# Attention with the values held still and the probabilities streamed, two heads on the column halves of the matrix engine

## The chip, the core and the metric

The kernel runs on one core of a Trainium2 chip. The core has a matrix engine (TensorE, PE in the rows; its weight loads are PEld), a vector engine (VectorE, DVE), a scalar engine (ScalarE, ACT), GpSimd (POOL), and a sync engine (SP) that issues the DMAs. Operands lie in SBUF, matmul results in PSUM, which has eight banks of 128 partitions by 512 fp32 numbers. A matmul holds one operand still in the array (the stationary one, loaded first) and streams the other through it (the moving one). The metric is the device time of one execution, in microseconds; less is better.

## The reference, cut to what matters

The program is one block of another design (a recurrence, a differential attention, an MLP) followed by two transformer layers on 256 tokens of width 1024. Each of the two layers is half an FFN, an attention of 16 heads of 64, and half an FFN again. The change is in those two attentions alone. Cut down, they compute:

```python
q, k, v = split(xn @ w_in, 3)                    # 16 heads of 64; xn is 256 x 1024
# layer 0, heads 0-7 (stick breaking)
z = q @ k.T * scale
between = sums of log_sigmoid(-z) over the later keys, strictly causal
out = exp(log_sigmoid(z) + between) @ v          # these weights need no normalisation
# layer 0, heads 8-15 ("moba": with 256 tokens there is one block, so plain causal softmax)
# layer 1, heads 0-7 ("forget": causal softmax, logits + c_q - c_k)
# layer 1, heads 8-15 ("dilated": softmax over window keys, each weighted by a count 1..3)
p = softmax(logits); out = p @ v
x = x + concat(out) @ w_out
```

## The kernel before, in words

The kernel is one long instruction stream for TensorE in an order fixed when the program is built; the other engines are placed around it by a scheduler. The dense products (weights in fp32, split into a high and a low part so that three one-pass matmuls replace an exact one, `mm3`) form the main stream. Attention is written as side streams (Python generators) that a planner, `Weave`, slips between the matmuls of the main stream. The planner keeps a clock `W.t` made of its own estimates (`mm` adds `2 * max(n, m) / 1.2` ns for an exact fp32 product with `m` stationary and `n` moving columns, times `share`); a side stream says how long it wants to be left alone (`yield 3.0` is 3 us by that clock) or what it waits for, and takes its PSUM bank with `sbank`.

The 16 heads of a layer come in four groups of four heads. For each group the main stream makes q and k (`queries`) and v (`values`), and side streams do the rest:

- `softmax_side`, one stream per group and per block `t` of 128 queries: logits by four matmuls, mask added by matmul, row maximum (DVE), exponent with row sums (ACT), transposes of the unnormalised probabilities on TensorE (L707) and their copy to SBUF (ACT, L709). Then the values product (L721 to L723): for each of four heads and each of `t + 1` blocks of 128 keys one exact fp32 matmul, whose stationary operand is the transposed 128 x 128 probability block and whose moving operand is the head's 64 columns of v. The output is 128 queries by 4 x 64. It is multiplied by the reciprocal sums into a tile `o` (DVE, L727), and `out_side` (L650) transposes `o` in two blocks back to a feature-major layout, from which `dst` copies it to `oT` or, for the last group, splits it for the output projection.
- `stick_group` with two `stick_pair` streams per group: the two heads of a pair each take three such matmuls (L771 to L773), the group's results are copied to two tiles `o` (ACT, L785), and each goes through `out_side`.

In the profile all matmuls but transposes carry line L287 and all transposes line L291, so the tiles tell them apart: `b<-v,w` is a values product, `b<-ident,o` a transpose of an output, `b<-ident,w` a transpose of probabilities (or of q and k), `b<-hi,hTh`, `lo,hTh` and `hi,hTl` are the three products of the main stream. An exact fp32 matmul leaves two records in the profile, a transpose one.

Of the kernel before, what the change touches and what calls it, by code (L numbers as in the profile page):

```python
# [7 lines left out]
F32 = mybir.dt.float32  # L8
# [4 lines left out]
AF = mybir.ActivationFunctionType  # L13
ALU = mybir.AluOpType
# [204 lines left out]
class Ker:  # L219
# [427 lines left out]
        self.w2.put(i, 0.0)  # L647
        return 0.8

    def out_side(self, o, dst):  # L650

        b = yield from self.sbank()
        for k in range(2):
            self.tr(b[1][:, k * 128:(k + 1) * 128], o[:, k * 128:(k + 1) * 128])
        dst(b[1][:, :256].rearrange("p (a b) -> p a b", b=128))
        self.sdrop(b, 1.6)

    def softmax_side(self, pool, t, wait, lhs, rhs, vm, mask, cnt, dst):

        nc = self.nc  # L660
# [23 lines left out]
        for par in range(2):  # L684
# [9 lines left out]
                    nc.vector.scalar_tensor_tensor(out=pp[:, i, :nk], in0=pp[:, i, :nk], scalar=1.0, in1=cnt[:, 256 - nk:], op0=ALU.mult, op1=ALU.mult, accum_out=l[:, h:h + 1])  # L694
                P[h] = pp[:, i]
            self.sdrop(bs[par], 2.2 + par)
        yield 3.0 if cnt is None else 4.2
        PT = {}
        blocks = [(h, b) for h in (0, 2, 1, 3) for b in range(t + 1)]
        pts = []  # L700
# [10 lines left out]
            self.w2.put(held.pop(0), 0.0)  # L711
        for i in held:
            self.w2.put(i, 0.0)
        rl = pool.tile([128, 4], F32, name="rl", tag="rl", bufs=4)
        nc.vector.reciprocal(out=rl, in_=l)
        yield [vm]
        yield 0.8
        vt = vm.res
        ab = yield from self.sbank()
        av = ab[1][:, :256].rearrange("p (h d) -> p h d", d=64)  # L720
        for h in (0, 2, 1, 3):  # L721
            for b in range(t + 1):
                self.mm(av[:, h], PT[h, b], vt[b][:, h * 64:h * 64 + 64], b == 0, b == t)  # L723
        for k in pts:
            self.w2.put(k, 0.0)
        o = pool.tile([128, 256], F32, name="o", tag="o", bufs=3)
        nc.vector.tensor_tensor(out=o.rearrange("p (h d) -> p h d", d=64), in0=av, in1=rl.unsqueeze(2).to_broadcast([128, 4, 64]), op=ALU.mult)  # L727
        self.sdrop(ab)
        yield 1.0
        yield from self.out_side(o, dst[t])  # L730
        return 1.6

    def stick_pair(self, pool, j, ab, wait, kT, qT, vm):

        nc, mm = self.nc, self.mm
        yield wait
        bs = yield from self.sbanks()
        hs = (2 * j, 2 * j + 1)
        zs = [b[1][:, :384] for b in bs]
        for a, b, first in ((0, 0, True), (128, 256, False)):  # L740
            for z, h in zip(zs, hs):
                mm(z[:, b:b + 256 - a], kT(h, a, a + 128), qT(h, a, 256), first, True, True, 0.5)
        diag = [b[1].rearrange("p (a k) -> p a k", k=256)[:, :, 0:128] for b in bs]
        self.add_mask(diag, self.A["stick"], lambda x: x.unsqueeze(1).to_broadcast([64, 2, 128]))
        sp = []
        for z in zs:
            e = pool.tile([128, 384], F32, name="e", tag="e", bufs=2)
            nc.scalar.activation(out=e, in_=z, func=AF.Abs)
            self.act_pinned(out=e, in_=e, func=AF.Exp, scale=-1.0)
            self.act_pinned(out=e, in_=e, func=AF.Ln, bias=1.0)  # L750
            i, w = yield from self.w2.get()
            nc.vector.scalar_tensor_tensor(out=w[:, :384], in0=z, scalar=0.0, in1=e, op0=ALU.max, op1=ALU.add)
            sp.append((i, w))
        yield 4.6
        for z, (i, w) in zip(zs, sp):
            mm(z[:, 0:256], self.A["nsuf"], w[:, 0:256], False, True, True)
            mm(z[:, 128:256], self.A["nones"], w[:, 256:384], False, True, True)
            mm(z[:, 256:384], self.A["nsuf"], w[:, 256:384], False, True, True)
            self.w2.put(i, 0.0)
        ws = []  # L760
        for b, z in zip(bs, zs):
            i, w = yield from self.w2.get()
            self.act_pinned(out=w[:, :384], in_=z, func=AF.Exp)
            self.sdrop(b, 1.0)
            ws.append((i, w))
        yield [vm]
        yield 1.6
        vt = vm.res
        for h, (i, w) in zip(hs, ws):
            vs = slice(h * 64, h * 64 + 64)  # L770
            mm(ab[:, 0, h], w[:, 0:128], vt[0][:, vs], True, True)  # L771
            mm(ab[:, 1, h], w[:, 128:256], vt[0][:, vs], True, False)
            mm(ab[:, 1, h], w[:, 256:384], vt[1][:, vs], False, True)  # L773
            self.w2.put(i, 0.0)

    def stick_group(self, pool, wait, kT, qT, vm, dst):
        b = yield from self.sbank()
        ab = b[1].rearrange("p (t h d) -> p t h d", t=2, d=64)
        heads = [self.W.spawn(self.stick_pair(pool, j, ab, wait, kT, qT, vm)) for j in range(2)]
        yield heads  # L780
        os = []
        for t in range(2):
            o = pool.tile([128, 256], F32, name="o", tag="o", bufs=3)
            os.append(o)
            self.nc.scalar.activation(out=o.rearrange("p (h d) -> p h d", d=64), in_=ab[:, t], func=AF.Copy)  # L785
        self.sdrop(b)
        yield 0.9
        for t in range(2):
            yield from self.out_side(os[t], dst[t])
        return 1.6  # L790

    def attn_layer(self, pool, hT, layer, after):
# [1070 lines left out]
```

## Time and profile before

| | us |
|---|---|
| median of 3 timed runs | 1516.84 (1516.67 to 1520.73) |
| the profiled execution | 1517.79 |
| its span, first to last instruction | 1516.0 |
| TensorE busy in the span | 1473.4 (97%) |
| VectorE, ScalarE busy | 927.7 (61%), 760.7 (50%) |
| attention of layer 0, and of layer 1 (with the norm before it) | about 680 to 812, and 1188 to 1320 |

A row of instructions names the source line, the engine, the operation, the tiles written and read, for TensorE the stationary shape as rows*columns and then the moving shape, and the count of records. Matmul records overlap, since they are pipelined, so the rate of a stream is read from the starts of its records, not from their lengths.

### The profile page before, as it was taken

Reading aid. Unit: us, or ns where it says so; the run is one execution under the profiler, and the core shown is the slowest. Engines: PE = TensorE matmul, PEld = TensorE weight load, DVE = VectorE, ACT = ScalarE, POOL = GpSimd, SP = SyncE. Lnnn points to the kernel's source line nnn. Section 1 sums busy time; section 2 is a strip of 40 time slices with the busy share of each in tenths; the row PEclk is TensorE's granted clock in tenths of the full one; section 3 lists DMA queues with packets and bytes.
Section 4 is the critical chain, followed back from the end, with each engine's and each line's share of the span. In section 5 each row is a group of like instructions: output and inputs, shape, how many; then the busy total and the mean of one; then the engine's idle time right before and its main releaser. Section 6 shows DMA issues by size and latency. Waiting matters only on the chain.

```text
span 1516.0 us, 22441 instructions
## 1 busy us (share of the span) xinstructions
PE 1473.4 (97%) x8804; PEld 1235.3 (81%) x8804; DVE 927.7 (61%) x1529; ACT 760.7 (50%) x1142; POOL 46.9 (3%) x70
## 2 busy tenths in 40 slices
PE   7899988999999999999999999999999999999999
PEld 6887767888888778887888888887888878888887
DVE  5885778755558755558546554565545787565552
ACT  6644445544446544436665444445444566464441
POOL 1120100000000000001100000000000010000000
PEclk9999999999999999999999999999999999999999
DMA  7233338655554765545434756547565444276551
GB/s 254 87 121 108 101 113 272 203 191 187 181 167 140 229 204 193 186 145 195 137 101 140 220 184 196 187 146 235 183 195 189 139 158 128 82 223 193 177 186 55
DMA packets 76298, 254.97 MB, mean 168 GB/s; under 512 B 11040, under 2 KB 13344, under 8 KB 76192
## 3 DMA queue, kind: packets, MB, share of 16 engines
q1 hardware_dynamic: 76192, 253.53, 51.8%
q8 instruction: 69, 1.13, 0.3%
q14 instruction: 37, 0.30, 0.1%
HBM read 252.45 MB, written 1.05 MB: 167 GB/s over the span
## 4 chain that ended last, share of the span: by engine, by line
PE 79%; DVE 7%; DMA 6%; ACT 5%; issue 2%; SPq 0%; POOL 0%; ACTq 0%; DVEq 0%; POOLq 0%
PE b L287 75%; DMA raw<-in_w_dram 5%; PE b L291 4%; DVE lo L374 3%; ACT hi L373 2%; DMA grow<-in_norm_mix_g_dram 0%; DMA stage<-in_consts_dram 0%; DMA lam<-in_lam_k_dram 0%; ACT L380 0%; DVE c L1141 0%; POOL rb L572 0%; DVE U L1269 0%; POOL rb L571 0%; DVE u L1138 0%; ACT e L384 0%
## 5 line engine op out<-in xcount | busy, mean ns | idle before, releaser
L374 DVE TENSOR_TENSOR lo<-raw,hi 128x1024 fp32r<-128x1024 f32 (+1 forms) x465 | 562.0, 1215 | 356.1 <-ACT hi L373 347.1
L373 ACT ACTIVATE hi<-raw 128x1024 fp32r<-128x1024 f32 (+1 forms) x465 | 486.0, 1050 | 415.8 <-PE b L287 207.1
L287 PE MATMUL b<-hi,hTh 128*128 128x512 f32 (+2 forms) x1312 | 495.6, 378 | 0.5 <-ACT hi L373 0.5
L287 PE MATMUL b<-lo,hTh 128*128 128x512 f32 (+2 forms) x1312 | 484.7, 369 | 0.8 <-DVE lo L374 0.8
L287 PE MATMUL b<-hi,hTl 128*128 128x512 f32 (+2 forms) x1312 | 484.9, 370 | 0.1
L287 PEld LDWEIGHTS b<-hi,hTl 128*128 128x128 f32 x1312 | 247.5, 189 | 43.1 <-DVE hTl L374 0.6
L287 PEld LDWEIGHTS b<-hi,hTh 128*128 128x128 f32 x1312 | 247.6, 189 | 42.0 <-issue 2.7
L287 PEld LDWEIGHTS b<-lo,hTh 128*128 128x128 f32 x1312 | 248.0, 189 | 40.0 <-DVE lo L374 1.7
L287 PE MATMUL b<-hi,aTh 128*128 128x512 f32 x480 | 191.4, 399 | 0.0
L287 PE MATMUL b<-lo,aTh 128*128 128x512 f32 x480 | 187.3, 390 | 0.0
L287 PE MATMUL b<-hi,aTl 128*128 128x512 f32 x480 | 187.2, 390 | 0.0
L287 PEld LDWEIGHTS b<-hi,aTl 128*128 128x128 f32 x480 | 90.2, 188 | 19.8
L287 PEld LDWEIGHTS b<-lo,aTh 128*128 128x128 f32 x480 | 90.3, 188 | 17.4
L287 PEld LDWEIGHTS b<-hi,aTh 128*128 128x128 f32 x480 | 90.2, 188 | 17.5
L471 ACT ACTIVATE a<-b,rsi_x 128x512 f32<-128x512 f32 (+1 forms) x52 | 34.4, 662 | 54.0 <-PE b L287 54.0
L373 ACT ACTIVATE aTh<-b 128x512 fp32r<-128x512 f32 (+1 forms) x64 | 36.3, 567 | 39.5 <-PE b L291 38.5
L473 DVE SCALAR_TENSOR_TENSOR a<-b,rsi_x,a 128x512 f32<-128x512 f32 (+1 forms) x52 | 37.3, 717 | 28.4 <-PE b L287 15.9
L287 PE MATMUL b<-hi,hT1h 128*128 128x512 f32 (+1 forms) x128 | 53.5, 418 | 0.0
L374 DVE TENSOR_TENSOR aTl<-b,aTh 128x512 fp32r<-128x512 f32 (+1 forms) x64 | 41.8, 653 | 17.2 <-ACT aTh L373 16.9
L287 PE MATMUL b<-lo,hT1h 128*128 128x512 f32 (+1 forms) x128 | 47.7, 372 | 0.6 <-DVE lo L374 0.6
L287 PE MATMUL b<-hi,hT1l 128*128 128x512 f32 (+1 forms) x128 | 47.4, 371 | 0.0
L374 DVE TENSOR_TENSOR hTl<-b,hTh 128x512 fp32r<-128x512 f32 (+1 forms) x48 | 29.2, 619 | 23.5 <-ACT hTh L373 23.5
(583 smaller groups left out, 1289.0 us busy)
## 6 DMA issues: line engine op xcount, KB each, us to landing
raw<-in_w_dram SPq DMA_DIRECT2D x446, 512.0 KB, 4.2
raw<-in_w_dram SPq DMA_DIRECT2D x16, 384.0 KB, 3.4
grow<-in_norm_ffn_dram SPq DMA_DIRECT2D x4, 512.0 KB, 5.0
x<-in_x_dram SPq DMA_DIRECT2D x4, 256.0 KB, 5.5
x<-in_x_dram SPq DMA_DIRECT2D x2, 512.0 KB, 4.3
grow<-in_norm_mix_dram SPq DMA_DIRECT2D x2, 512.0 KB, 4.5
out_dram<-x SPq DMA_DIRECT2D x4, 256.0 KB, 2.0
raw<-in_w_dram SPq DMA_DIRECT2D x2, 396.0 KB, 3.5
```

The costliest lines, as they stand in the source:

```text
L287: self.nc.tensor.matmul(out=out, lhsT=lhsT, rhs=rhs, start=start, stop=stop, skip_group_check=skip)
L291: self.nc.tensor.transpose(out=out, in_=src, identity=self.ident)
L373: self.nc.scalar.activation(out=hi, in_=src, func=AF.Copy)
L374: self.nc.vector.tensor_tensor(out=lo, in0=src, in1=hi.bitcast(F32), op=ALU.subtract)
L471: nc.scalar.activation(out=a[t], in_=p, func=AF.Silu if kind == "swiglu" else AF.Relu, scale=hT[t].r)
L473: nc.vector.scalar_tensor_tensor(out=a[t], in0=p, scalar=hT[t].r, in1=a[t], op0=ALU.mult, op1=ALU.mult)
```

## The change

The values product is turned round: v becomes the stationary operand (128 keys by the 64 columns of one head) and the transposed probabilities the moving one (128 columns, or 256 in the stick groups). The output is then feature-major: 64 partitions by 128 queries. Two heads of a pair are written to the two partition halves of one PSUM bank, so each matmul addresses 64 of the array's 128 columns. Since the sums are then along the wrong axis of the output, the probabilities are divided before they are transposed: one `reciprocal` and four scalings by a row factor, two on ACT and two on DVE. `o`, its scaling and copies, and `out_side` are gone; `dst` reads the PSUM bank directly. The planner's clock gets `share` 0.5 for the new matmuls, and the wait before the transposes is 1 us longer.

```diff
--- before.py
+++ after.py
@@ -647,14 +647,6 @@
         self.w2.put(i, 0.0)
         return 0.8
 
-    def out_side(self, o, dst):
-
-        b = yield from self.sbank()
-        for k in range(2):
-            self.tr(b[1][:, k * 128:(k + 1) * 128], o[:, k * 128:(k + 1) * 128])
-        dst(b[1][:, :256].rearrange("p (a b) -> p a b", b=128))
-        self.sdrop(b, 1.6)
-
     def softmax_side(self, pool, t, wait, lhs, rhs, vm, mask, cnt, dst):
 
         nc = self.nc
@@ -694,7 +686,15 @@
                     nc.vector.scalar_tensor_tensor(out=pp[:, i, :nk], in0=pp[:, i, :nk], scalar=1.0, in1=cnt[:, 256 - nk:], op0=ALU.mult, op1=ALU.mult, accum_out=l[:, h:h + 1])
                 P[h] = pp[:, i]
             self.sdrop(bs[par], 2.2 + par)
-        yield 3.0 if cnt is None else 4.2
+        rl = pool.tile([128, 4], F32, name="rl", tag="rl", bufs=4)
+        nc.vector.reciprocal(out=rl, in_=l)
+        for h in (0, 2, 1, 3):
+            p = P[h][:, :nk]
+            if h % 2:
+                nc.vector.tensor_scalar(out=p, in0=p, scalar1=rl[:, h:h + 1], scalar2=None, op0=ALU.mult)
+            else:
+                nc.scalar.activation(out=p, in_=p, func=AF.Copy, scale=rl[:, h:h + 1])
+        yield 4.0 if cnt is None else 5.2
         PT = {}
         blocks = [(h, b) for h in (0, 2, 1, 3) for b in range(t + 1)]
         pts = []
@@ -711,26 +711,23 @@
             self.w2.put(held.pop(0), 0.0)
         for i in held:
             self.w2.put(i, 0.0)
-        rl = pool.tile([128, 4], F32, name="rl", tag="rl", bufs=4)
-        nc.vector.reciprocal(out=rl, in_=l)
         yield [vm]
         yield 0.8
         vt = vm.res
         ab = yield from self.sbank()
-        av = ab[1][:, :256].rearrange("p (h d) -> p h d", d=64)
-        for h in (0, 2, 1, 3):
-            for b in range(t + 1):
-                self.mm(av[:, h], PT[h, b], vt[b][:, h * 64:h * 64 + 64], b == 0, b == t)
+        av = ab[1][:, :256].rearrange("p (j q) -> p j q", q=128)
+        for b in range(t + 1):
+            for j in range(2):
+                for par in range(2):
+                    h = 2 * j + par
+                    self.mm(av[64 * par:64 * par + 64, j], vt[b][:, h * 64:h * 64 + 64], PT[h, b], b == 0 and j == 0, b == t and j == 1, True, 0.5)
         for k in pts:
             self.w2.put(k, 0.0)
-        o = pool.tile([128, 256], F32, name="o", tag="o", bufs=3)
-        nc.vector.tensor_tensor(out=o.rearrange("p (h d) -> p h d", d=64), in0=av, in1=rl.unsqueeze(2).to_broadcast([128, 4, 64]), op=ALU.mult)
-        self.sdrop(ab)
-        yield 1.0
-        yield from self.out_side(o, dst[t])
+        dst[t](av)
+        self.sdrop(ab, 1.6)
         return 1.6
 
-    def stick_pair(self, pool, j, ab, wait, kT, qT, vm):
+    def stick_pair(self, pool, j, ab, begun, wait, kT, qT, vm):
 
         nc, mm = self.nc, self.mm
         yield wait
@@ -766,27 +763,23 @@
         yield [vm]
         yield 1.6
         vt = vm.res
-        for h, (i, w) in zip(hs, ws):
-            vs = slice(h * 64, h * 64 + 64)
-            mm(ab[:, 0, h], w[:, 0:128], vt[0][:, vs], True, True)
-            mm(ab[:, 1, h], w[:, 128:256], vt[0][:, vs], True, False)
-            mm(ab[:, 1, h], w[:, 256:384], vt[1][:, vs], False, True)
+        first = not begun
+        begun.append(j)
+        for b in range(2):
+            for par, (i, w) in enumerate(ws):
+                h = 2 * j + par
+                mm(ab[64 * par:64 * par + 64, j, 128 * b:256], vt[b][:, h * 64:h * 64 + 64], w[:, 256 * b:256 + 128 * b], first and b == 0, b == 1 and not first, True, 0.5)
+        for i, w in ws:
             self.w2.put(i, 0.0)
 
     def stick_group(self, pool, wait, kT, qT, vm, dst):
         b = yield from self.sbank()
-        ab = b[1].rearrange("p (t h d) -> p t h d", t=2, d=64)
-        heads = [self.W.spawn(self.stick_pair(pool, j, ab, wait, kT, qT, vm)) for j in range(2)]
-        yield heads
-        os = []
-        for t in range(2):
-            o = pool.tile([128, 256], F32, name="o", tag="o", bufs=3)
-            os.append(o)
-            self.nc.scalar.activation(out=o.rearrange("p (h d) -> p h d", d=64), in_=ab[:, t], func=AF.Copy)
-        self.sdrop(b)
-        yield 0.9
-        for t in range(2):
-            yield from self.out_side(os[t], dst[t])
+        ab = b[1].rearrange("p (j q) -> p j q", q=256)
+        begun = []
+        yield [self.W.spawn(self.stick_pair(pool, j, ab, begun, wait, kT, qT, vm)) for j in range(2)]
+        for t in range(2):
+            dst[t](ab[:, :, t * 128:t * 128 + 128])
+        self.sdrop(b, 1.6)
         return 1.6
 
     def attn_layer(self, pool, hT, layer, after):
```

In the built program the DMA queue and GpSimd have the same instructions in the same order as before. TensorE's stream differs only inside the two attentions: 96 values matmuls become 88 (24 + 48 of the softmax streams as before, 16 instead of 24 of the stick streams), and 32 transposes of outputs are gone. The 88 stand in 15 places, 8 with four and 7 with eight, between other work each time.

The first place is the first values product of layer 0 (heads 8 to 11, queries 0 to 127). TensorE before; `w__6941` holds the transposed probabilities:

```order
L287 MATMUL b<-hi,hTl 128x512
L287 MATMUL b<-v,w__6941 128x64 x4
L287 MATMUL b<-hi,hTh 128x512
L287 MATMUL b<-lo,hTh 128x512
L287 MATMUL b<-hi,hTl 128x512
...
L291 MATMUL b<-ident,o 128x128 x2
```

TensorE now, at the same place (`w__6950` is the same tile under another number):

```order
L287 MATMUL b<-hi,hTl 128x512
L287 MATMUL b<-w__6950,v 64x128 x4
L287 MATMUL b<-hi,hTh 128x512
L287 MATMUL b<-lo,hTh 128x512
L287 MATMUL b<-hi,hTl 128x512
```

The four matmuls now write 64 partitions by 128 columns instead of 128 by 64, they alternate between the lower and the upper half of the bank, and the two transposes that followed are gone.

The second place is the first stick group of layer 0, where the two pairs finish. TensorE before (`w__7199` and `w__7201` are the weights of the two heads of a pair, `w__7212` and `w__7214` of the other pair):

```order
L287 MATMUL b<-v,w__7199 128x64 x3
L287 MATMUL b<-v,w__7201 128x64 x3
L287 MATMUL b<-hi,hTh 128x512
...
L287 MATMUL b<-v,w__7212 128x64 x3
L287 MATMUL b<-v,w__7214 128x64 x3
```

TensorE now:

```order
L287 MATMUL b<-w__7197,v 64x256
L287 MATMUL b<-w__7199,v 64x256
L287 MATMUL b<-w__7197,v 64x128
L287 MATMUL b<-w__7199,v 64x128
L287 MATMUL b<-hi,hTh 128x512
...
L287 MATMUL b<-w__7210,v 64x256
L287 MATMUL b<-w__7212,v 64x256
L287 MATMUL b<-w__7210,v 64x128
L287 MATMUL b<-w__7212,v 64x128
```

Six matmuls of a pair have become four, two of them 256 columns wide, and the two heads alternate.

The third place is the start of layer 1's attention, where little work is ready. TensorE before, from the transposes of q and k (`w__11120`) over those of the first probabilities (`w__11211`, `w__11212`, dilated heads) to the next logits (`qkT`):

```order
L291 MATMUL b<-ident,w__11120 128x128 x4
L287 MATMUL b<-hi,hTh 128x512
L287 MATMUL b<-lo,hTh 128x512
L287 MATMUL b<-hi,hTl 128x512
L291 MATMUL b<-ident,w__11211 128x128 x2
L291 MATMUL b<-ident,w__11212 128x128 x2
L287 MATMUL b<-qkT 128x256 x4
```

TensorE now (`w__11088` are q and k, `w__11179` the first of the probabilities):

```order
L291 MATMUL b<-ident,w__11088 128x128 x4
L287 MATMUL b<-hi,hTh 128x512
L287 MATMUL b<-lo,hTh 128x512
L287 MATMUL b<-hi,hTl 128x512
...
L287 MATMUL b<-qkT 128x256 x4
...
L291 MATMUL b<-ident,w__11179 128x128 x2
```

The transposes of the probabilities have moved behind the next logits and their masks, and six matmuls of the main stream instead of three stand ahead of those logits.

## Rows read from the trace of the kernel before

**Rows 1.** Page, busy time of each engine; granted TensorE clock in 40 slices (tenths).

```profile
PE 1473.4 (97%) x8804; PEld 1235.3 (81%) x8804; DVE 927.7 (61%) x1529; ACT 760.7 (50%) x1142; POOL 46.9 (3%) x70
...
PEclk9999999999999999999999999999999999999999
```

**Rows 2.** Page, chain of work that ended last, by engine.

```profile
PE 79%; DVE 7%; DMA 6%; ACT 5%; issue 2%; SPq 0%; POOL 0%; ACTq 0%; DVEq 0%; POOLq 0%
```

**Rows 3.** Stretches: length; busy PE, PEld, DVE, ACT, POOL; clock, DMA share, GB/s.

```profile
680.00:812.00 132.00, 128.82 (x812) 111.23 (x811) 75.97 (x121) 80.42 (x165) 9.16 (x8) 0.99 0.39 128
1188.00:1320.00 132.00, 127.89 (x798) 110.38 (x797) 91.69 (x210) 77.71 (x168) 8.81 (x8) 1.00 0.40 130
```

**Rows 4.** Waits of TensorE in layer 0, then layer 1: total us, times, longest.

```profile
PE b L291 <- DVE qss L558: 2.0, 1, 2.0
...
PE b L291 <- DVE w__11212 L694: 0.6, 1, 0.6
```

**Rows 5.** Timeline of TensorE, layer 0: start us, length us, instruction, stationary, moving.

```profile
714.71 0.40 PE L287 MATMUL b<-hi,hTl 128*128 128x512 f32 x1
714.95 1.00 PE L287 MATMUL b<-v,w__6941 128*128 128x64 f32 x8
...
716.07 0.39 PE L287 MATMUL b<-lo,hTh 128*128 128x512 f32 x1
...
716.99 0.39 PE L287 MATMUL b<-hi,hTl 128*128 128x512 f32 x1
717.22 0.38 PE L291 MATMUL b<-ident,o 128*128 128x128 f32 x2
...
717.68 0.39 PE L287 MATMUL b<-lo,hTh 128*128 128x512 f32 x1
```

**Rows 6.** Timeline of TensorE in the recurrence, 64-column matmuls between full ones.

```profile
130.39 0.40 PE L287 MATMUL b<-hi,hT1l 128*128 128x512 f32 x1
130.72 0.45 PE L287 MATMUL b<-UV,G 128*64 128x64 f32 x4
131.00 0.39 PE L287 MATMUL b<-S,AR 128*64 128x128 f32 x2
131.22 0.39 PE L287 MATMUL b<-UV,G 128*64 128x64 f32 x4
131.45 0.38 PE L287 MATMUL b<-S,AR 128*64 128x128 f32 x2
...
132.10 0.40 PE L287 MATMUL b<-lo,hT1h 128*128 128x512 f32 x1
```

**Rows 7.** Timeline in the recurrence, weight loads beside matmuls.

```profile
141.66 0.20 PEld L287 LDWEIGHTS b<-S,AR 128*64 128x64 f32 x2
141.72 0.39 PE L287 MATMUL b<-S,AR 128*64 128x128 f32 x2
141.83 0.36 PEld L287 LDWEIGHTS b<-UV,G 128*64 128x64 f32 x4
```

**Rows 8.** Timeline of TensorE, layer 0, logits on the row halves.

```profile
712.86 1.13 PE L287 MATMUL b<-qkT 64*128 64x256 f32 x8
713.82 0.38 PE L287 MATMUL b<-cb_causal,cb_identb 64*128 64x256 bf16 x4
```

**Rows 9.** Timeline of TensorE, layer 0, an exact matmul with 256 moving columns.

```profile
736.43 0.59 PE L287 MATMUL b<-w__7124,c_nsuf 128*128 128x256 f32 x2
736.86 0.38 PE L287 MATMUL b<-w__7124,c_nones 128*128 128x128 f32 x2
```

**Rows 10.** Groups by line: busy us, mean ns of one, idle before it.

```profile
L374 DVE TENSOR_TENSOR lo<-raw,hi 128x1024 fp32r<-128x1024 f32 (+1 forms) x465 | 562.0, 1215 | 356.1 <-ACT hi L373 347.1
...
L727 DVE TENSOR_TENSOR o<-b,rl 128x256 f32<-128x256 f32 x12 | 5.1, 422 | 4.9 <-PE b L287 4.7
...
L715 DVE RECIPROCAL rl<-l 128x4 f32<-128x4 f32 x12 | 2.1, 175 | 5.3 <-ACT w__7427 L384 1.5 <-ACT w__12156 L384 1.4 <-ACT w__11606 L384 1.4
...
L614 ACT ACTIVATE w__6994<-b,rsi_x 128x256 f32<-128x256 f32 x1 | 0.5, 474 | 0.0
```

## The prediction

> **What bounds the kernel now.** I read the page's busy times first, then the chain, then the two attentions as stretches, then the waits, and last the timeline of the places that change. TensorE is busy 97% of the span and its clock is at the full level in every slice [rows 1]; 79% of the chain that ended last is TensorE [rows 2]. That is an average over stages, so the attentions are read by themselves: in each, TensorE is busy 128 of 132 us, while DVE and ACT have 58 to 70% at most and the DMA engines 40% [rows 3]. The few idle microseconds of TensorE there stand at the start of a layer and end on the preparation of q and k (2.0 us in layer 0); the only wait that ends on a softmax is one of 0.6 us [rows 4]. So a microsecond of TensorE work taken out of an attention should shorten the program by about a microsecond, as long as nothing new comes late.
>
> **What goes on TensorE.** The unit to compare with is the main stream: from 716.07 to 716.99 four records start, 0.23 us each [rows 5]. From 714.71 to 716.07 lie two such steps and the four values matmuls of four heads (eight records): 1.36 - 0.46 = 0.90 us, or 0.225 us a matmul [rows 5]. Before the change there are 24 of 96 such matmuls in fours: 6 softmax streams with one key block (24 matmuls), 6 with two (48), 4 pairs of stick heads with six (24). 96 / 4 x 0.90 = 21.6 us. The transposes of the outputs: from 716.99 to 717.68 lie two steps and two transposes, 0.69 - 0.46 = 0.23 us [rows 5]; 32 of them, 16 x 0.23 = 3.7 us. Together 25.3 us go.
>
> **What comes on TensorE.** The new shape, 64 stationary columns and 128 moving ones, is in the trace, in the recurrence: `S,AR` takes 0.22 us for its two records (131.00 to 131.22), as long as the old shape, because now the moving side sets the pace [rows 6]. With 256 moving columns an exact matmul takes 0.43 us (736.43 to 736.86) [rows 9]. So one matmul by itself gains nothing; the gain is that two heads, on different column halves, run at the same time. No row shows two column halves side by side: in the recurrence a run stays on one half. The nearest rows are the row halves: eight records of logits with 256 moving columns, four matmuls of 0.43 us, take 0.96 us from 712.86 to the next kind at 713.82, where one after the other they would take 1.72 [rows 8, 9]. The bounds are therefore 0.22 us a pair (at the same time) and 0.44 (in turn). I take the first, since the rows next to it run in parallel, and since two exact streams together ask for no more than the trace already shows: one has 128 columns in 0.11 us a record [rows 6], so two of them have 256, and the main stream's 512 columns in 0.23 us are the same rate [rows 5].
> The softmax streams then have 6 x 2 + 6 x 4 = 36 pairs x 0.22 = 7.9 us, the stick pairs 4 x (0.43 + 0.22) = 2.6 us, together 10.5.
> TensorEngine Tiling (Array Packing) in the Trainium skill says under Key Properties that different tiles can load and multiply in parallel; TensorE: Matmul & The Clock Gate, also of the Trainium skill, gives in Part 3 (Packing small matmuls) a measured speedup of 2.38 for three column tiles. No run here shows either. By 2.38 out of 3 a pair would cost 0.28 us, the 10.5 would be 13.2, and the gain 2.7 us less.
>
> **What the switch costs.** Going to 64 columns and back is not free. From 130.39 to 132.10 lie two main steps (0.46), eight records of `UV,G` at 0.23 us per four, and two `S,AR` at 0.22 (0.90 in all): 1.71 - 0.46 - 0.90 = 0.35 us are left, between the last full matmul and the second one after [rows 6]. A values product of the old shape has no such remainder: its eight records take eight times the 0.11 us. The order of the new program has 15 such places, 15 x 0.35 = 5.25 us. For four matmuls that means 2 x 0.22 + 0.35 = 0.79 against 0.90: nearly the whole gain is eaten; for eight, 1.23 against 1.80. A bound from the other side is the same remainder with two halves to load, 0.05 more each (the first four `UV,G` take 0.28 instead of 0.23 [rows 6]): 6.0 us.
> The sum on TensorE: 25.3 - 10.5 - 5.25 = 9.5 us less.
>
> **What moves on the other engines.** DVE loses 12 `o` scalings of 0.42 us [rows 10] and gets 24 of a probability tile, which lies in SBUF and is at most as large; ACT gets 24, at most 0.47 us each by the nearest row [rows 10], and loses four copies. In the attentions ACT rises by at most 6 us per 132 and DVE by less than 3, and neither comes near full [rows 3]. No DMA moves.
> The new wait is that the transposes of the probabilities need the reciprocal, which needs all four row sums: 0.18 us on DVE, then two scalings on ACT, 0.94 us, while DVE does its two beside [rows 10], about 1.1 us per stream. On ACT the next weight halves and exponents queue behind the waiting scalings, on DVE the reciprocal can stand behind a low-half split of 1.2 us [rows 10]. What hides this is the main stream: between logits and transposes the new order still has at least 18 full steps of it or twice as many half ones (4 us), and the planner waits 1 us more. The bounds are 0 and 1.7 us in each of 12 streams. I take 0.8 us over all, one more wait like the 0.6 us one [rows 4], since the third place of the order keeps its first transposes behind the next logits. The tail loses the way over `o` and transposes, about what the scalings add ahead of it: nothing.
> 9.5 - 0.8 = 8.7 us: the span goes from 1516.0 to 1507.3, and with the 1.8 us outside it the execution from 1517.8 to 1509.1. The median of the runs is 0.95 us below the profiled execution, so I say 1508.1.
>
> **The rivals.**
> *In turn.* The two halves do not overlap. For: no row shows it. Against: row halves do overlap [rows 8]. The 10.5 doubles, TensorE gains 25.3 - 21.0 - 5.25 = -1.0, with 0.8 us of waits 1516.84 + 1.8 = 1518.6.
> *Loads in the open.* The halves multiply together, but no load can go under a running matmul of the other half, as both use the same rows. Each of the 176 records then shows its load, 0.05 us (the first four `UV,G` [rows 6]), 8.8 us if loads go in turn and 4.4 if two go together: the gain falls to 0.7 or 5.1, less 0.8: 1512.5 to 1516.9. Against it, a load of 64 columns starts at 141.83 while a matmul on the same 128 rows that started at 141.72 still runs [rows 7]; but that is one half.
> The Trainium skill's TensorE: Matmul & The Clock Gate, Part 3, has this rule: loads overlap running matmuls only when the row group differs. By it the change would be worth almost nothing; the trace disagrees for a single half.
> *The scaling on the path, slower.* The place is between exponent and transposes of every softmax stream. Each costs 1.1 us of chain and half of the time a split in front of the reciprocal (0.6): 12 x 1.7 = 20.4 us, 1516.84 - 9.5 + 20.4 = 1527.7. It decides from 0.8 us per stream on, where it eats the 9.5. For: DVE is 70% busy in layer 1 [rows 3], and one stream was late already [rows 4]. Against: the steps of main stream that stand between.
> *It does not do what it says.* The transposes of outputs and eight stick matmuls are gone in the order, so this is the first rival with another cause.
>
> **How the numbers follow.** Forecast 0.75, in turn 0.10, loads in the open 0.10, scaling on the path 0.05. The forecast's own range is 1504.5 to 1512: below by no waits, no new remainder where two places lie close, and the end of the tail; above by 6.0 us for the switches and 3 us of waits. The range runs from 1504.5 to 1517.0, which takes in the loads in the open and leaves out the first and the last rival and a little of the forecast's lower end. Less than 0.3% (4.5 us) can't be told from no change in this kernel: faster means below 1512.3. The forecast gives 0.70 of that and the loads in the open 0.03; the same gets the rest of these two and the halves in turn, 0.22; slower 0.05.
>
> **What would show it.** In the timeline after, records of `b<-w,v` start in pairs a few ns apart, four matmuls take 0.45 us and eight 0.9, with 0.35 us left around each place; rows `b<-ident,o` are gone, the span's difference lies within the two attentions, and waits of TensorE on probability tiles stay under 2 us. Pairs 0.1 us apart mean the first rival, gaps of 0.05 us between pairs the second, and idle TensorE before `b<-ident,w` the third. A clock below its full level after such a wait would make my sum wrong too.

## The result, and the profile after

The changed kernel takes 1507.81 us (median of 6, 1506.06 to 1512.65) where the kernel before, run beside it, takes 1516.76 (1514.89 to 1520.73): a ratio of 0.9945, 95% interval 0.9933 to 0.9957. That is 9.0 us less. The forecast was 1508.1.

The page of the changed kernel: busy time of TensorE with its share and records, its granted clock in 40 slices, and the chain that ended last.

```profile
PE 1463.1 (97%) x8756; PEld 1219.0 (81%) x8756; DVE 929.2 (62%) x1541; ACT 769.5 (51%) x1162; POOL 46.5 (3%) x70
...
PEclk9999999999999999999999999999999999999999
...
PE 76%; DVE 9%; DMA 7%; ACT 5%; issue 2%; SPq 0%; POOL 0%; ACTq 0%; DVEq 0%; POOLq 0%
```

Against [rows 1] TensorE has 10.3 us less to do and 48 records fewer, DVE 1.5 us more and ACT 8.8. The span is 1504.9 us, 11.1 less than before, but not all of that is the change's. A stretch that fits both kernels runs from the last gate product of the half FFN ahead of an attention (the start of L473 on DVE) to the first activation of the half FFN behind it (the start of L471 on ACT). First the two attentions of the kernel before, then those of the changed one; columns as in [rows 3].

```profile
662.48:825.55 163.07, 159.89 (x959) 136.92 (x958) 99.12 (x172) 95.85 (x188) 9.16 (x8) 0.99 0.42 137
1171.63:1334.07 162.44, 158.34 (x945) 135.59 (x944) 113.69 (x260) 92.84 (x192) 8.81 (x8) 1.00 0.41 133
```

```profile
660.43:819.25 158.82, 154.10 (x928) 127.89 (x927) 99.67 (x176) 98.05 (x192) 9.15 (x8) 1.00 0.44 141
1164.30:1323.21 158.91, 153.97 (x930) 128.32 (x929) 115.87 (x268) 98.81 (x209) 8.99 (x8) 1.00 0.42 136
```

Length less busy time is idle time of TensorE. The attentions became 4.25 and 3.53 us shorter, 7.8 in all: busy time fell by 10.2, idle time rose by 2.4 (from 3.2 + 4.1 to 4.7 + 4.9). The other 3.3 us of the span lie where nothing changed (at 662 the changed kernel is already 2.05 us ahead; the part up to there, which no edit touches, takes 658.4 to 664.6 us in the fourteen profiles of this study). Two more profiles of the changed kernel have spans of 1509.6 and 1505.1 us but attentions of 317.80 and 315.69 us in all, against 317.73 here. So from here on the attentions are compared, and the changed kernel stands for the mean of its three profiles: 317.1 us, 308.0 busy, 9.0 idle; the kernel before: 325.5, 318.2, 7.3.

The record also has the mean granted clock of TensorE, as a share of full speed, for every timed execution. The span times what this clock lacks of 1 is an estimate of the time that the lower clock took. It is 8.0 us on average in the 74 executions of the kernel before that stand beside the later runs, and 7.5 in the 17 of the changed kernel. Of the 9.1 us between their mean times the clock thus makes 0.5, and 8.6 remain. With this estimate taken off, the mean spans are 1507.8 and 1499.2 us; below they are called the means with the clock off. The kernel before gives 1507.5 to 1508.8 by chip, so a difference of 1 us between such means tells little.

What TensorE waits for in the attention of layer 0, then of layer 1, in the changed kernel (total us, times, longest):

```profile
PE b L291 <- DVE qss L558: 1.9, 1, 1.9
PE b L291 <- DVE w__6784 L574: 1.2, 1, 1.2
...
PE b L291 <- ACT w__6869 L696: 0.3, 1, 0.3
```

```profile
PE b L291 <- ACT w__11575 L696: 1.7, 1, 1.7
PE b L287 <- ACT qkT L645: 1.6, 1, 1.6
...
PE b L291 <- DVE w__11678 L694: 0.2, 1, 0.2
```

L694 and L696 are the new scalings: 2.2 us of waits in place of the 0.6 of [rows 4]. The new 1.2 us for `w__6784` has another cause, told in the last section.

The places that changed. The timeline of TensorE in the changed kernel at the place of [rows 5], four matmuls (start, length, instruction):

```profile
714.50 0.39 PE L287 MATMUL b<-hi,hTl 128*128 128x512 f32 x1
714.82 0.66 PE L287 MATMUL b<-w__6950,v 128*64 128x128 f32 x8
...
715.75 0.40 PE L287 MATMUL b<-lo,hTh 128*128 128x512 f32 x1
```

From 714.50 to 715.75 are 1.25 us: two main steps 0.46, two pairs 0.44, and 0.35 for the place. Before it was 1.36. With eight matmuls the records can be seen one by one:

```profile
720.78 0.40 PE L287 MATMUL b<-hi,hTl 128*128 128x512 f32 x1
721.11 0.32 PE L287 MATMUL b<-w__7018,v 128*64 128x128 f32 x1
721.11 0.32 PE L287 MATMUL b<-w__7025,v 128*64 128x128 f32 x1
721.27 0.27 PE L287 MATMUL b<-w__7018,v 128*64 128x128 f32 x1
...
721.38 0.27 PE L287 MATMUL b<-w__7018,v 128*64 128x128 f32 x1
...
722.47 0.39 PE L287 MATMUL b<-lo,hTh 128*128 128x512 f32 x1
```

`w__7018` holds the even heads and `w__7025` the odd ones. Two records start together, the next two 0.16 us later, and each two after them 0.11. 720.78 to 722.47 are 1.69 us. In the kernel before a place with eight matmuls looked like this (layer 1, the last group):

```profile
1303.95 0.39 PE L287 MATMUL b<-hi,hTl 128*128 128x512 f32 x1
1304.18 1.00 PE L287 MATMUL b<-v,w__12263 128*128 128x64 f32 x8
1305.01 1.06 PE L287 MATMUL b<-v,w__12270 128*128 128x64 f32 x8
...
1306.19 0.39 PE L287 MATMUL b<-lo,hTh 128*128 128x512 f32 x1
```

1303.95 to 1306.19 are 2.24 us; the place shown above took 2.25. Over all places, measured in this way and with equal numbers of main steps, 6.0 us went. The 32 output transposes, at the 0.23 us a pair of [rows 5], are another 3.7; no experiment took them alone.

### The profile page after: what moved, and what is told of

Its sections match the earlier page's. It is cut to its first block, busy times and chain, and to the rows that moved or that the text cites. A ratio compares the mean times of both kernels' runs of the same rounds, so it can differ in the third digit from the quotient of the medians.

```text
span 1504.9 us, 22374 instructions
## 1 busy us (share of the span) xinstructions
PE 1463.1 (97%) x8756; PEld 1219.0 (81%) x8756; DVE 929.2 (62%) x1541; ACT 769.5 (51%) x1162; POOL 46.5 (3%) x70
## 4 chain that ended last, share of the span: by engine, by line
PE 76%; DVE 9%; DMA 7%; ACT 5%; issue 2%; SPq 0%; POOL 0%; ACTq 0%; DVEq 0%; POOLq 0%
PE b L287 72%; DMA raw<-in_w_dram 6%; PE b L291 4%; DVE lo L374 3%; ACT hi L373 3%; DMA grow<-in_norm_mix_g_dram 0%; DMA stage<-in_consts_dram 0%; DMA lam<-in_lam_k_dram 0%; ACT L380 0%; DVE c L1134 0%; DVE G L1231 0%; DVE qn L562 0%; POOL rb L572 0%; DVE m L679 0%; DVE u L1131 0%
## 5 line engine op out<-in xcount | busy, mean ns | idle before, releaser
L471 ACT ACTIVATE a<-b,rsi_x 128x512 f32<-128x512 f32 (+1 forms) x52 | 34.5, 663 | 51.5 <-PE b L287 51.5
L473 DVE SCALAR_TENSOR_TENSOR a<-b,rsi_x,a 128x512 f32<-128x512 f32 (+1 forms) x52 | 37.3, 717 | 27.3 <-PE b L287 14.7
L373 ACT ACTIVATE hTh<-b 128x512 fp32r<-128x512 f32 (+1 forms) x48 | 25.3, 540 | 35.0 <-PE b L291 25.6
```

The lines of the kernel that those rows point to most:

```text
L373: self.nc.scalar.activation(out=hi, in_=src, func=AF.Copy)
L471: nc.scalar.activation(out=a[t], in_=p, func=AF.Silu if kind == "swiglu" else AF.Relu, scale=hT[t].r)
L473: nc.vector.scalar_tensor_tensor(out=a[t], in0=p, scalar=hT[t].r, in1=a[t], op0=ALU.mult, op1=ALU.mult)
```

## The experiments

Each experiment changes one thing in the changed kernel (e9 changes e5). "Attentions" is the sum of the two stretches; the ratio is to the kernel before on the same chip. The last column is the time that a slow clock took: 4 us times what the granted clock lacks of 1, over stretches of 4 us where it lacks more than 0.02; the last section tells of it.

| kernel | median us | ratio [95%] | attentions | busy | idle | lost to the clock |
|---|---|---|---|---|---|---|
| before | 1516.8 | 1 | 325.5 | 318.2 | 7.3 | 1.6 |
| changed, three times | 1507.8, 1509.0, 1507.4 | 0.9945, 0.9943, 0.9930 | 317.1 | 308.0 | 9.0 | 0 |
| e1, halves grouped | 1512.5 | 0.9968 [0.9952, 0.9984] | 318.7 | 310.4 | 8.3 | 0 |
| e8, one half | 1515.1 | 0.9981 [0.9966, 0.9995] | 324.3 | 316.1 | 8.2 | 1.7 |
| e2, no scaling | 1506.6 | 0.9930 [0.9908, 0.9953] | 313.5 | 306.6 | 6.9 | 0 |
| e3, more places | 1514.8 | 0.9990 [0.9977, 1.0003] | 324.9 | 315.9 | 9.0 | 1.7 |
| e4, stick old | 1512.0 | 0.9964 [0.9949, 0.9979] | 318.9 | 310.1 | 8.8 | 0 |
| e5, merged, twice | 1507.7, 1506.1 | 0.9923 [0.9902, 0.9944], 0.9925 [0.9905, 0.9944] | 313.6, 316.2 | 305.3, 308.1 | 8.3, 8.1 | 0, 1.7 |
| e6, wait longer | 1507.0 | 0.9925 [0.9903, 0.9947] | 316.6 | 308.4 | 8.2 | 1.7 |
| e7, wait shorter | 1516.6 | 0.9986 [0.9971, 1.0002] | 321.1 | 308.5 | 12.6 | 0 |
| e9, merged, layer 1 later | 1506.9 | 0.9931 [0.9918, 0.9944] | 315.7 | 307.1 | 8.5 | 1.7 |

**e1: the halves grouped.**

```diff
-        for b in range(t + 1):
-            for j in range(2):
-                for par in range(2):
+        for par in range(2):
+            for b in range(t + 1):
+                for j in range(2):
```

> The changed kernel with one edit: inside each of the 15 places all values matmuls of the first column half are issued first, then all of the second, so neighbours in the order lie on the same half. Nothing else moves. My theory (the gain of 9.5 us on TensorE comes from two halves running at the same time, in the order of issue): only the last matmul of the one half and the first of the other can still meet, so the 10.5 us of pairs nearly double: 9 to 10.5 us slower than the changed kernel (1507.8), so 1517 to 1518.5, no faster than the kernel before. In the timeline the records of a place start 0.11 us apart, eight of them in 0.8 us instead of 0.4. Rival (the engine starts a matmul whose half is free ahead of earlier ones, or the gain comes from the transposes and the order): no change, 1507 to 1509, and pairs as before.

Neither theory held. Places with four matmuls did not change at all (1.25 us from the last main step to the second after, records in pairs 14 ns apart). Places with eight went from 1.69 to 2.17. The timeline of e1 at the same place as above:

```profile
721.07 0.76 PE L287 MATMUL b<-w__7018,v 128*64 128x128 f32 x5
721.56 0.32 PE L287 MATMUL b<-w__7025,v 128*64 128x128 f32 x1
721.67 0.27 PE L287 MATMUL b<-w__7018,v 128*64 128x128 f32 x1
...
721.78 0.27 PE L287 MATMUL b<-w__7018,v 128*64 128x128 f32 x1
...
721.88 0.27 PE L287 MATMUL b<-w__7018,v 128*64 128x128 f32 x1
```

In the program all eight records of `w__7018` come first. Yet the first of `w__7025` starts at 721.56, ahead of the last three of `w__7018`. So a matmul can overtake earlier ones of the other half, by three records here; beyond that the halves stand in a row. The time says the same: the place takes 2.17 us, where all matmuls in a row take 2.55 (e8). In an order by half, four matmuls overlap fully and eight by a part. Six such places x 0.48 are 2.9 us; busy time rose by 2.4. The test did not separate what it was made for, so e8 was added.

**e8: one half.** It leaves out a part of the result: to judge by its start flags, the second key block of one head in four replaces the first one's sum. No instruction is fewer.

```diff
-        av = ab[1][:, :256].rearrange("p (j q) -> p j q", q=128)
+        av = ab[1][0:64].rearrange("p (h q) -> p h q", q=128)
...
-                    self.mm(av[64 * par:64 * par + 64, j], vt[b]...
+                    self.mm(av[:, h], vt[b]...
```

> The changed kernel, but in the 12 softmax streams all four heads go to the first column half (each head its own 128 columns of the bank), so no two of these matmuls can run at the same time; the order on TensorE, the 15 places and the stick groups stay, and the bank is copied out in two pieces, one for each partition half. My theory (the halves running together carry the gain): 36 pairs of 0.22 us become 72 matmuls in turn, 7.9 us slower than the changed kernel, 1515 to 1517, with records 0.11 us apart: 16 of them in 1.6 us instead of 0.8. Rival (the gain comes from the transposes that are gone and the shorter way behind the product): 0 to 2 us slower, below 1510.

The records now stand in a row, two of them (one matmul) in 0.22 us. The timeline of e8, eight matmuls of a place in layer 0:

```profile
718.32 0.40 PE L287 MATMUL b<-hi,hTl 128*128 128x512 f32 x1
718.64 0.43 PE L287 MATMUL b<-w__7019,v 128*64 128x128 f32 x2
718.91 0.38 PE L287 MATMUL b<-w__7026,v 128*64 128x128 f32 x2
...
720.87 0.39 PE L287 MATMUL b<-lo,hTh 128*128 128x512 f32 x1
```

718.32 to 720.87 are 2.55 us instead of 1.69, and a place of four takes 1.67 instead of 1.25: 6 x 0.86 + 6 x 0.43 = 7.7 us, for 7.9 expected. The ratios give 5.5 (0.0036 of 1517), the attentions 7.2, of which 1.7 are a slow clock, and the means with the clock off 7.6 (1506.8 against 1499.2). Side by side is what carries the gain in the softmax streams; without it the product in its new shape is dearer than the old one (2.55 against 2.25), since it pays for the place too.

**e3: more places.**

```diff
                     self.mm(av[64 * par:64 * par + 64, j], vt[b]...
+                if (b, j) != (t, 1):
+                    yield 0.3
```

(and one such `yield` in the stick pairs)

> The changed kernel, but after each step of two values matmuls a side stream gives way for 0.3 us of the planner's clock, so that main products come in between: 35 places instead of 15 with the same matmuls (34 stretches of 64-column form instead of 15). My theory (0.35 us is lost at each going to 64 columns and back): 19 or 20 x 0.35 = 6.6 to 7.0 us slower than the changed kernel, 1514.4 to 1514.8. Rival 1 (the remainder of a place is not the change of form but something paid once per bank or per stream): 0 to 1 us. Rival 2 (most of the place's remainder is the fill of the pairs and of the exact form, which short places hide): about half, 3 us.

Two matmuls that stand alone, in the timeline of e3:

```profile
723.48 0.39 PE L287 MATMUL b<-hi,hTl 128*128 128x512 f32 x1
723.80 0.32 PE L287 MATMUL b<-w__7018,v 128*64 128x128 f32 x1
723.80 0.32 PE L287 MATMUL b<-w__7025,v 128*64 128x128 f32 x1
...
724.50 0.39 PE L287 MATMUL b<-lo,hTh 128*128 128x512 f32 x1
```

723.48 to 724.50 are 1.02 us: 0.46 + 0.22 + 0.34. The price of a place does not depend on how much stands in it, and rival 2 falls. By the ratios e3 costs 6.8 us more than the changed kernel (0.0045 of 1517), as expected. The means with the clock off differ by 6.9. Busy time rose by 7.9, of which 1.7 are a slow clock that this profile happened to have in layer 1; 6.2 over 19 or 20 places are 0.31 to 0.33 us.

**e4: the stick groups as before.** The functions `stick_pair` and `stick_group` are those of the kernel before, with `out_side`.

> The changed kernel with the stick groups of layer 0 as in the kernel before (probabilities stationary, copies to o, transposes of the outputs); the softmax groups keep the change. My theory: 24 values matmuls 5.4 us and 8 transposes 0.9 come back, 2.6 us of pairs and 3 places x 0.35 go: 2.7 us slower than the changed kernel, about 1510.5, all of it in layer 0. Rival 1 (stick pairs gain nothing, since matmuls with 256 moving columns fill the engine alone): 0. Rival 2 (they carry half of the gain): 4.5 us, 1512.3.

By the ratios 2.9 us slower, by busy time 2.0, all in layer 0 (156.3 us busy instead of 154.1; layer 1 153.7 and 153.9). The expected 2.7 lies between, and the records of the places and the eight transposes give 2.6. Half of the gain (4.5 us), as rival 2 has it, is outside what the profile shows; the means with the clock off differ by 3.8, so the times alone don't exclude it.

**e2: without the scalings.**

```diff
-        rl = pool.tile([128, 4], F32, name="rl", tag="rl", bufs=4)
-        nc.vector.reciprocal(out=rl, in_=l)
-        for h in (0, 2, 1, 3):
...
-                nc.scalar.activation(out=p, in_=p, func=AF.Copy, scale=rl[:, h:h + 1])
```

> The changed kernel without the reciprocal and the four scalings of the probabilities in each of the 12 softmax streams (it leaves out the normalisation); the planner's waits stay, so the order on TensorE is the same. My theory (scaling costs only the waits that the profile shows on probability tiles, 0.3 + 1.7 + 0.2 us): 1.0 to 2.2 us faster than the changed kernel, 1505.5 to 1507, and those three waits gone or under 0.5 us in total. Rival 1 (scaling costs nothing, other waits take the place): 0. Rival 2 (scaling delays splits and copies behind it on ACT and DVE, so that its price is hidden in other waits): 4 us or more, below 1504.

It leaves out the normalisation. The three waits are gone, idle time fell by 2.1 us, the ratios give 2.3 (their intervals overlap with the changed kernel's), the means with the clock off 1.3, and the attentions 3.6 (1.5 of it busy time, which this edit shouldn't touch, so take it as the scatter of one profile). The price of the scalings is about 2 us: my theory's range holds, and rival 2 is out.

Where the longest of these waits comes from shows in ACT's and DVE's rows of the changed kernel, around 1246 (start, length, engine, instruction, what it waited for):

```profile
1245.19 0.21 ACT L384 ACTIVATION_READ_ACCUMULATOR w__11576<-b,m 128x1 f32 x1
1245.29 0.61 ACT L555 ACTIVATE sq<-b 128x512 f32<-128x512 f32 x1
1245.44 0.18 DVE L690 RECIPROCAL rl<-l 128x4 f32<-128x4 f32 x1 [0.27 <-ACT w__11576 L384]
1245.65 0.62 DVE L694 TENSOR_SCALAR w__11576<-w__11576,rl 128x256 f32<-128x256 f32 x2
1245.77 0.92 ACT L696 ACTIVATE w__11575<-w__11575,rl 128x256 f32<-128x256 f32 x2
1246.34 0.84 PE L291 MATMUL b<-ident,w__11575 128*128 128x128 f32 x4 [1.66 <-ACT w__11575 L696]
```

The last row sum is there at 1245.40, the last scaled block at 1246.69: reciprocal, a square of another stream that stands ahead on ACT (L555) and delays the first scaling there by at most 0.15 us (1245.62 to 1245.77), two scalings. The kernel before transposed each head as soon as its exponent was done; now the first transpose needs all four sums.

**e6 and e7: the wait before the transposes**, 1 us longer and 1 us shorter (`yield 5.0 ... 6.2` and `yield 3.0 ... 4.2`).

> The changed kernel with 5.0 and 6.2 instead of 4.0 and 5.2 us of the planner's clock between the scalings and the first transposes of the probabilities. If the price of the scaling (2 us of waits on probability tiles in the profile, up to 3.6 us less time in the attentions without it) is lateness at the transposes, most of it goes: 1.5 to 2.5 us faster, about 1506, the waits on L694 and L696 below 0.5 us. Rival (the price is on ACT and DVE, where other work queues behind the scalings): no change, or later streams wait more.

> The changed kernel with 3.0 and 4.2 us, as the kernel before had. If lateness at the transposes is the price: 1 us less cover in 12 streams, waits on L694 and L696 grow from 2.2 to between 4 and 10 us, and the kernel is 2 to 8 us slower, less 0.7 for 13 places instead of 15. Rival (the main stream between logits and transposes covers it anyway): no change.

The waits of e7 in layer 1, then those of e6:

```profile
PE b L291 <- ACT w__11179 L696: 2.7, 1, 2.7
PE b L291 <- ACT w__11575 L696: 2.6, 1, 2.6
...
PE b L291 <- ACT w__11671 L696: 0.9, 1, 0.9
PE b L291 <- DVE w__11180 L694: 0.3, 1, 0.3
```

```profile
PE b L287 <- ACT qkT L645: 2.5, 2, 1.4
```

With 1 us less cover the waits on scaled tiles in layer 1 grow from 1.9 to 6.5 us and idle time by 3.6; by the ratios the kernel is 6.2 us slower. The waits make only a part of that: the twelve executions of e7 lost 11.7 us to the clock by the estimate above, against 7.5 in the changed kernel, and the means with the clock off differ by 3.7 us (1502.9 against 1499.2), as much as the idle time rose. So the longer wait of the change is worth some 4 us by itself, and the rest of the 6.2 goes with the clock. That the longer waits in e7 bring the lower clock is not shown, since its one profile has none of it in the attentions. With 1 us more, the waits on L694 and L696 are gone, but logits wait for q and k (L645) instead, idle time falls by 0.8 us only, and the median is not to be told from the changed kernel's. Both the theory of lateness and its rival are right by a part. The planner's `share` of 0.5, another part of the change, was not varied.

**e5: fewer places.** The values product of both query blocks is made by the second stream, both stick pairs of a group together.

```diff
+        if mate and t == 0:
+            mate.res = (PT, pts)
+            self.W.finish(mate, 0.8)
+            return 0.8
         yield [vm]
         yield 0.8
+        if mate:
+            yield [mate]
+            ts, parts[0] = [0, 1], mate.res[0]
...
```

> The changed kernel with fewer places: for the first three groups of a layer the values product of both query blocks is made together by the second stream, and both stick pairs of a group together, 9 places instead of 15 with the same matmuls. Theory of a price per place (0.35 us): 6 x 0.35 = 2.1 us faster, 1505 to 1506.5, both layers. Rival (what is held longer, the work slots and the bank, makes the next stream late): waits of TensorE in the attentions grow by 2 us or more, and no gain.

> e5_merged once more, beside the changed kernel on the same chip. If the 4.2 us that its first profile shows less in the two attentions are the kernel's and not the single execution's: attentions together 3.5 to 5 us shorter than in the changed kernel again, median 2 to 5 us below the changed kernel's. If most of it was one lucky execution: 1 to 2 us, the price of six places.

> The changed kernel a third time, as the other side of that comparison: two attentions together 317 to 318.5 us, TensorE busy 308 to 309 us of it, as in its first two profiles.

> The changed kernel once more, on the chip of e9 and with as many rounds, so that both stand beside the same runs of the kernel before: 7 to 10.5 us below the kernel before, the two attentions together 7 to 9 us shorter; if a second profile of the same kernel differs from the first by more than 1 us in TensorE's idle time in the attentions, waits of that size in single profiles tell nothing.

The nine places take 1.7 us less than the fifteen, measured as above; 2.1 was expected. The attentions are 3.5 and 0.9 us shorter than the mean of the changed kernel, and 2.6 in the second profile when its slow clock is taken off. By the ratios it takes 0.8 us less than the changed kernel run beside it, and 3.3 less than that in its first runs, with overlapping intervals. It beats the kernel before clearly (by 0.75%) and the changed kernel probably, by 1 to 3 us, which these runs can't assure. The rival fell: the waits in the attentions did not grow (idle time 8.3 and 8.1 us against 9.0).

The repeats of the changed kernel: attentions 317.8 and 315.7 us, the second below the range that was expected; the waits on L694 and L696 came back as 2.2 us both times, so they are the kernel's own. Idle time was 9.7, 9.2 and 8.3 us in the three profiles; first and third differ by 1.4, more than the 1 us that I had set, most of it in the wait for `qss` (1.9 and 0.9). A difference of that size in the idle time of single profiles shows nothing by itself.

**e9: e5 with a longer wait in layer 1.**

> e5_merged with 1 us of the planner's clock more before the transposes of the probabilities in layer 1 alone (e6 showed TensorE's waits on scaled probabilities gone there, but new waits in layer 0). Theory: the 9 places keep e5's gain and layer 1 loses its 1.8 us of waits on probability tiles: the attentions together 3 to 5 us shorter than in the changed kernel, about 1503.5 as a median, 3 to 5 us below the changed kernel run beside it. Rival: what is held longer makes the logits or the values product late instead (waits on L645 or L709 grow by as much): no better than e5.

It is no better than e5, as the rival says, but not for the rival's reason: the waits on L645 did not grow (1.3 us, 1.4 in e5) and none on L709 appeared. The wait on scaled tiles did not go, it moved to the next stream (`w__11671`), and a slow clock followed. The median is 2.1 us below that of the changed kernel beside it (1509.0), where the theory had 3 to 5. TensorE's timeline of e9, and under it two stretches of the same run:

```profile
1251.21 0.63 PE L291 MATMUL b<-ident,w__11608 128*128 128x128 f32 x4
1253.20 0.62 PE L291 MATMUL b<-ident,w__11671 128*128 128x128 f32 x2 [1.36 <-ACT w__11671 L696]
1254.07 0.69 PE L291 MATMUL b<-ident,w__11672 128*128 128x128 f32 x2 [0.26 <-DVE w__11672 L694]
...
1255.60 0.42 PE L287 MATMUL b<-w__11656,v 128*64 128x128 f32 x1
1255.81 0.42 PE L287 MATMUL b<-w__11656,v 128*64 128x128 f32 x1
```

```profile
1251.00:1255.00 4.00, 2.35 (x13) 1.37 (x14) 3.42 (x13) 1.38 (x4) 0.00 (x0) 0.86 0.36 109
1255.00:1259.00 4.00, 4.00 (x32) 3.19 (x28) 0.57 (x7) 1.05 (x3) 0.00 (x0) 0.72 0.47 158
```

The pairs are 0.21 us apart instead of 0.11; 0.14 and 0.28 of 4 us are 1.7 us lost.

## Why the prediction was right, step by step

**What goes and comes on TensorE: right.** A place of four was to go from 0.90 to 0.79 us and one of eight from 1.80 to 1.23; they went down by 0.11 and 0.56. The records give 6.0 + 3.7 = 9.7 us, forecast 9.5. Busy time in the attentions fell by 10.2 on average; 1.6 of this is a slow clock in the kernel before (below), so 8.6 by that view. Why the two views differ by 1.1 us stays open. The bounds of the unknown pair, 0.22 and 0.44 us, were both seen: the first in the changed kernel, the second in e8. The 0.28 us a pair, an estimate from the Trainium skill's speedup for three column tiles (TensorE: Matmul & The Clock Gate, Part 3), did not come: the pairs take 0.22.

**The switch: right.** 0.35 us at each place, and the same for a place with one pair (e3).

**The waits: too small by their own rows, not by idle time.** I took 0.8 us for the scalings on the ground that one more wait like the 0.6 us one would appear. The waits on probability tiles rose from 0.6 to 2.2 us, so by 1.6, and without the scalings about 2 us come back. Idle time in the attentions rose by 1.7 (three profiles), but 1.2 of this is the wait for `w__6784`, which goes with the clock (below); 0.5 is left, because the waits for `qss` and for q and k became shorter. So the term lies between 0.5 and 1.6 us. The chain was seen (all four sums, then 1.1 us; 1.29 at the place above); not seen was that the kernel before took the heads one by one, and, for 0.15 us at most, that ACT has another stream's square in front. My sign for this step, "under 2 us in total", was missed by 0.2.

**The clock: read wrongly.** I took it to be at the full level in every slice, from the nines of [rows 1]. A nine is a slice of 38 us with 90% or more; the mean granted clock of that profile is 0.995. It did not decide the result (0.5 of 9.1 us).

**The place of the difference: within the attentions, 7.7 to 9.8 us in three profiles**, as said; the 3.3 us outside in the first one are scatter, in the second the same parts are 1.3 us slower than before, behind 3.4 us more of low clock ahead of 520 us.

**The rivals.** *In turn* is out by the pairs, and e8 shows that it would have taken most of the gain away. *Loads in the open* is out: within a half the records are 0.109 us apart, as they are in e8, so no load shows between them. Only the second record comes 0.05 us later than that (0.16 at 721.27), once in a place and inside its 0.35. The rule of the Trainium skill behind it (the same page and part: loads overlap running matmuls only when the row group differs) does not hold here: both halves use all 128 rows, and at 721.16 a load of `w__7018,v` starts while, by its record, the matmul of 721.11 to 721.43 still runs. *Scaling on the path* was the right place and a far too high price: one stream of twelve waits 1.7 us and two others 0.2 and 0.3; e7 shows that it is the longer wait which keeps it there.

So the total of 1508.1 came out by a TensorE term that was right within 1 us and a wait that was at most 0.8 us too small, both inside the scatter of the medians. That the first median lies within 0.3 us of it is luck: the three runs of the changed kernel lie 9.0, 8.5 and 11.5 us below the kernel before beside them.

## What to carry to other kernels

Price a change of the array's form as a fixed cost for each place where it happens (0.35 us here) and a rate beside it, and read both off a place of the trace that already does it: small products gain only when several stand together. When a normalisation moves ahead of a step that used to take heads one by one, look for the last input it now needs and at what stands in front of it on its engine. Judge a change of half a per cent by the stretches that it touches, with a second profile of the same kernel beside them.

## What the runs showed of the hardware that was not expected

**Matmuls overtake.** In e1 a record of the second half starts at 721.56, before three earlier records of the first half (721.67 to 721.88). The Trainium skill says of packed tiles that matmuls start and end strictly in program order (TensorE: Matmul & The Clock Gate, Part 3); this trace differs in the starts, and the measurement decides.

**A slow clock in single profiles, and a wait that hides it.** In the kernel before:

```profile
700.00:704.00 4.00, 1.99 (x18) 1.81 (x17) 3.98 (x6) 2.52 (x4) 2.56 (x2) 1.00 0.70 235
704.00:708.00 4.00, 4.00 (x27) 3.31 (x26) 3.56 (x7) 1.82 (x4) 0.00 (x0) 0.59 0.58 172
```

After a wait of 2.0 us for `qss` TensorE's clock is at its lower level (1.2 GHz) for a part of the next stretch: 0.41 x 4 = 1.6 us lost. The page's slices of 38 us don't show it. In the three profiles of the changed kernel the same wait (1.9, 1.8 and 0.9 us) was not followed by a lower clock; TensorE came to the next transposes sooner and waited 1.1 to 1.2 us for `w__6784` there. e6 and the second e5 bear this out: they have the lower clock behind a `qss` wait of 2.1 and 2.0 us, and no wait for `w__6784`; the other eleven profiles have that wait and no lower clock ahead of it. The length of the `qss` wait does not decide alone: in e3 it is 2.0 us as well, and the clock stayed at its upper level. So 1.6 us less busy time and 1.2 us more idle time in layer 0 belong to the clock and not to the change. Of the fourteen profiles of this study six have one such stretch in the attentions, each of 1.6 or 1.7 us, and none of the three of the changed kernel does; ahead of 520 us all fourteen have two to four of them. What decides when it comes was not tried and stays open.
